# A hybrid attention and SSD layer on one core: TensorE's order in the SSD phase written out in the source, decay clamp moved to ScalarE

## The chip, the core and the metric

One NeuronCore of a Trainium2 chip runs the whole step. The metric is device time in microseconds, from three runs of the kernel before: 3272.0, 3275.4 (the median) and 3277.58. PE is TensorE's matmul, PEld its weight load, DVE VectorE, ACT ScalarE, POOL GpSimd, SP the queue from which all DMAs are issued here.

## The reference

The input is a prompt of 2048 tokens and a sample group of 8 x 8 tokens, width 1024. One projection of the normalised input gives queries, keys, values, gates and the SSD's inputs. Beside a windowed attention stands a Mamba-2 branch (4 groups of 8 heads, state 128), scanned in chunks of 128 tokens:

```python
a_cs = jnp.cumsum(dts * A, axis=2)
seg = a_cs[:, :, :, None] - a_cs[:, :, None]
Lm = jnp.exp(jnp.where(causal, seg, -jnp.inf))
cb = jnp.einsum('bclgn,bcsgn->bclsg', Cs, Bs)
y_diag = jnp.einsum('bclsg,bclsgh,bcsghp->bclghp', cb, Lm, dx)
states = jnp.einsum('bclgn,bclgh,bclghp->bcghpn', Bs, decay_to_end * dts, xs)
# h = h * chunk_decay + states, chunk after chunk
y_off = jnp.einsum('bclgn,bcghpn,bclgh->bclghp', Cs, h_prev, jnp.exp(a_cs))
```

x, B and C come from a causal convolution of width 4 and a silu; the SSD's output is multiplied by silu(z) and normalised by group. Both branches are projected, gated, added and projected once more.

## The kernel before, in words

The prompt is cut into 4 blocks of 512 tokens. Three phases follow each other in one program: `phase_t1` (norm, attention projections, attention), `phase_s` (SSD) and `phase_t2` (the gates, the output projections and the sample group's small work). Every fp32 operand of a projection is split into two fp32r parts, and three products of the parts are summed, so one output tile of 128 x 512 takes 8 x 3 matmuls (`proj_w`, L181).

`phase_s` goes over 16 pairs of block and group. For each, `proj_group` makes ten projection tiles: B, C, four of x (all six through `conv_tile`, whose L742 and L743 on ACT take a tile out of PSUM and whose three L748 on DVE do the convolution) and four of z (L814, L815). Block 0 carries the sample's 64 columns too; there each tile is two matmul streams of 288 columns in two of the three PSUM buffers `mm`. Weights are loaded for two tiles at a time by `wload`, rounded on ACT (L147) and subtracted on DVE (L148). `load_h` fetches a block's eight `hT` tiles.

`ssd_group` then does, for B and C of all four chunks, transposes (L826) and C by B (L832), and for each chunk: the decay matrix L (DMA of the sums to `AB`, eight DVE clamps L843, Exp L844 on ACT, times `cbm` on POOL L845); `po`, C by the carried state H (L854); transposes of x (L858), `dx` and `wx` (L861, L862); `py`, the product with L (L866); `ws` split on ACT and POOL (L868, L869); `st`, the chunk's state (L872); the new H on DVE (L879); the output (L881 to L885). A group ends with squares and their sum (L887 to L897). `dt_block` makes a block's step sizes by a softplus of some twenty small DVE operations and three matmuls (L767 to L769).

The order of instructions on each engine is not the source's: a planner with a cost model of its own lists them, on all engines and across phases. It lays SSD matmuls of one group between projection matmuls of the next, often in the middle of a tile, and it lays projections of block 0 between the last attention matmuls of `phase_t1`. Each engine runs its list strictly in that order, and an instruction whose input is late holds up all behind it.

Of the kernel before, what the change touches and what calls it, by code (L numbers as in the profile page):

```python
# [9 lines left out]
F32 = mybir.dt.float32  # L10
F32R = mybir.dt.float32r
AF = mybir.ActivationFunctionType
# [5 lines left out]
P = 128  # L18
# [57 lines left out]
def build(tc, nc, a, o, seq, phases=("T1", "S", "T2"), dbg=None):  # L76
# [629 lines left out]
    def phase_s():  # L706
        with ExitStack() as es:
# [50 lines left out]
            def dt_block(b):  # L758
# [5 lines left out]
                V.tensor_tensor(dA, dt, A_bc.unsqueeze(1).to_broadcast([P] + sh), ALU.mult)  # L764
                dA2 = dA.rearrange("p c h -> p (c h)")
# [17 lines left out]
            def proj_group(b, g, hT):  # L783
                xcp = xcps[(4 * b + g) % 2]
                xT = xcp.tile([P, 4, TB], F32, name="xT", tag="xT")
                BT = xcp.tile([P, TB], F32, name="BT", tag="BT")
                CT = xcp.tile([P, TB], F32, name="CT", tag="CT")
                zs = xcp.tile([P, 4, TB], F32, name="zs", tag="zs")
                cb, cc = OFF_B + P * g, OFF_C + P * g
                smp = b == sb  # L790
                _, hl = wload([(0, w_in[:, cb : cb + P]), (P, w_in[:, cc : cc + P])])
                st = sample_tile(smp)
                for i, (ct, out) in enumerate(((16 + g, BT), (20 + g, CT))):
                    pcs = prompt_pieces(proj_w(mmp, hl, i * P, hT, smp), st[:, i] if smp else None)
                    conv_tile(pcs, ct, out)
                    if smp:
                        SY.dma_start(xs_d[:, ct], st[:, i])
                for i in range(2):
                    c = 512 * g + 256 * i
                    _, hl = wload([(0, w_in[:, OFF_X + c : OFF_X + c + 256])])  # L800
                    st = sample_tile(smp)
                    for j in range(2):
                        pcs = prompt_pieces(proj_w(mmp, hl, j * P, hT, smp), st[:, j] if smp else None)
                        conv_tile(pcs, 4 * g + 2 * i + j, xT[:, 2 * i + j])
                    if smp:
                        SY.dma_start(xs_d[:, 4 * g + 2 * i : 4 * g + 2 * i + 2], st)
                for i in range(2):
                    c = 512 * g + 256 * i
                    _, hl = wload([(0, w_in[:, OFF_ZS + c : OFF_ZS + c + 256])])
                    st = sample_tile(smp)  # L810
                    for j in range(2):
                        th = cp.tile([P, TB], F32, name="th", tag="th")
                        for ps, lo, n in prompt_pieces(proj_w(mmp, hl, j * P, hT, smp), st[:, j] if smp else None):
                            A.activation(th[:, lo : lo + n], ps, AF.Tanh, scale=0.5)  # L814
                            V.scalar_tensor_tensor(  # L815
                                out=zs[:, 2 * i + j, lo : lo + n], in0=th[:, lo : lo + n], scalar=1.0, in1=ps,
                                op0=ALU.add, op1=ALU.mult,
                            )
                    if smp:
                        SY.dma_start(zs_d[:, 4 * g + 2 * i : 4 * g + 2 * i + 2], st)  # L820
                return xT, BT, CT, zs

            def ssd_group(b, g, xT, BT, CT, zs, dt, acs, dec, wd):
                tr = trp.tile([P, NT, P], F32, name="tr", tag="tr")
                for c in range(NT):
                    PE.transpose(tr[:, c], BT[:, c * P : (c + 1) * P], ident)  # L826
                Bt = ck.tile([P, 2, NT, P], F32R, name="Bt", tag="Bt", bufs=1)
                split(Bt[:, 0], Bt[:, 1], tr)
                pcb = trp.tile([P, NT, P], F32, name="tr", tag="tr")
                for c in range(NT):  # L830
                    sl = slice(c * P, (c + 1) * P)
                    PE.matmul(pcb[:, c], BT[:, sl], CT[:, sl], start=True, stop=True)  # L832
                cbm = ck.tile([P, NT, P], F32, name="cbm", tag="cbm")
                V.tensor_tensor(cbm, pcb, tri.unsqueeze(1).to_broadcast([P, NT, P]), ALU.mult)  # L834
                for c in range(NT):
                    first = b == 0 and c == 0
                    sl = slice(c * P, (c + 1) * P)
                    hc = slice(c * 32 + 8 * g, c * 32 + 8 * g + 8)
                    AB = lp.tile([P, 8, P], F32, name="AB", tag="AB")
                    SY.dma_start(AB.rearrange("p h l -> p (h l)"), ac_d[b][hc].rearrange("h l -> (h l)").partition_broadcast(P))  # L840
                    L = lp.tile([P, 8, P], F32, name="L", tag="L")
# [3 lines left out]
                    G.tensor_tensor(L, L, cbm[:, c].unsqueeze(1).to_broadcast([P, 8, P]), ALU.mult)  # L845
                    if not first:
                        EB = lp.tile([P, 4, P], F32, name="EB", tag="EB")
                        for hl in range(2):
                            src = ac_d[b][hc].rearrange("(i l) t -> l i t", l=2)[hl]
                            SY.dma_start(EB[64 * hl : 64 * hl + 64], src.partition_broadcast(64))  # L850
                        A.activation(EB, EB, AF.Exp)
                        po = yop.tile([P, 4, P], F32, name="po", tag="po")
                        for i in range(4):
                            PE.matmul(po[:, i], H[g][:, i * P : (i + 1) * P], CT[:, sl], start=True, stop=True)  # L854
                        V.tensor_tensor(EB, po, EB, ALU.mult)
                    tr = trp.tile([P, 8, 64], F32, name="tr", tag="tr")
                    for i in range(4):
                        PE.transpose(tr[:, 2 * i : 2 * i + 2].rearrange("p h d -> p (h d)"), xT[:, i, sl], ident)  # L858
                    dx = ck.tile([P, 8, 64], F32, name="dx", tag="dx")
                    wx = ck.tile([P, 8, 64], F32, name="wx", tag="wx", bufs=1)  # L860
                    V.tensor_tensor(dx, tr, dt[:, hc].unsqueeze(2).to_broadcast([P, 8, 64]), ALU.mult)  # L861
                    V.tensor_tensor(wx, tr, wd[:, hc].unsqueeze(2).to_broadcast([P, 8, 64]), ALU.mult)  # L862
                    py = yp.tile([P, 4, P], F32, name="py", tag="py")
                    for i in range(4):
                        for hl in range(2):
                            PE.matmul(py[64 * hl : 64 * hl + 64, i], dx[:, 2 * i + hl], L[:, 2 * i + hl], start=True, stop=True)  # L866
                    ws = ck.tile([P, 2, 8, 64], F32R, name="ws", tag="ws", bufs=1)
                    A.copy(ws[:, 0], wx)  # L868
                    G.tensor_tensor(ws[:, 1], wx, ws[:, 0].bitcast(F32), ALU.subtract)  # L869
                    pst_ = stp.tile([P, 8, 64], F32, name="st", tag="st")  # L870
                    for n, (x, y) in enumerate(SPLIT3):
                        PE.matmul(pst_, Bt[:, x, c], ws[:, y], start=n == 0, stop=n == 2)  # L872
                    Hg = H[g].rearrange("p (h d) -> p h d", h=8)
                    if first:
                        V.tensor_copy(Hg, pst_)
                    else:
                        hd = ck.tile([P, 8, 64], F32, name="hd", tag="hd", bufs=1)
                        G.tensor_tensor(hd, Hg, dec[:, hc].unsqueeze(2).to_broadcast([P, 8, 64]), ALU.mult)
                        V.tensor_tensor(Hg, pst_, hd, ALU.add)  # L879
                    u = xT[:, :, sl]  # L880
                    G.tensor_tensor(u, u, Dcol[:, 4 * g : 4 * g + 4].unsqueeze(2).to_broadcast([P, 4, P]), ALU.mult)  # L881
                    V.tensor_tensor(u, py, u, ALU.add)  # L882
                    if not first:
                        G.tensor_tensor(u, u, EB, ALU.add)
                    V.tensor_tensor(zs[:, :, sl], zs[:, :, sl], u, ALU.mult)  # L885
# [8 lines left out]
                for i in range(2):  # L894
                    PE.matmul(pss, onesr, thl[:, i], start=i == 0, stop=i == 1)
# [421 lines left out]
```

## Time and profile before

| | |
|---|---|
| median of three runs | 3275.4 us (3272.0 to 3277.58) |
| profiled execution | span 3273.9 us; no other time of this execution is known |
| PE, PEld | 3130.4 us (96%), 2656.9 us (81%) |
| DVE, ACT, POOL | 2234.8 (68%), 1308.2 (40%), 1045.0 us (32%) |
| granted TensorE clock | 0.987 on the mean |

The 1.5 us between the span and the median are what lies around the span, and scatter. The busy shares are means over three unlike phases. A busy PE is not a PE at its pace, since matmuls overlap and their ends are modelled; how fast a stretch runs is read from the starts of matmuls that follow each other.

### The profile page before, as it was taken

What the parts mean: (1) busy time and instruction counts of PE and PEld (TensorE: products, weight loads), DVE (VectorE), ACT (ScalarE), POOL (GpSimd) and SP (SyncE); (2) the same over time, 40 slices, a digit from 0 to 9 for tenths busy, and PEclk for the clock granted to TensorE, in tenths of its full rate; (3) what the DMA queues carried; (4) which work ended last, traced back from release to release, by engine and by line L of the source; (5) the groups of instructions that cost most, each with busy time, mean ns of one, the idle gap of its engine ahead of it and who ended that gap; (6) DMA issues with size and microseconds to landing.
All of it is one profiled execution on the core that took longest, in us unless ns stands there. A gap on an engine that the chain in (4) does not pass through costs nothing.

```text
span 3273.9 us, 49350 instructions
## 1 busy us (share of the span) xinstructions
PE 3130.4 (96%) x19038; PEld 2656.9 (81%) x19038; DVE 2234.8 (68%) x3777; ACT 1308.2 (40%) x2334; POOL 1045.0 (32%) x965
## 2 busy tenths in 40 slices
PE   6999999999989999998999999999999999999999
PEld 5978787878878877776777777788877799999888
DVE  3777768678887798989888898555555554334433
ACT  3555535456344344434444444332333333222322
POOL 1534343443445455556554555200211110000000
PEclk8999999999999999999999999999999999999999
DMA  6544425323433444444344433444764574345443
GB/s 210 156 134 124 128 73 169 106 70 124 130 122 110 154 125 135 126 156 133 116 143 155 127 118 119 154 141 117 229 184 142 131 226 147 97 135 168 132 116 101
DMA packets 472788, 448.76 MB, mean 137 GB/s; under 512 B 33808, under 2 KB 420520, under 8 KB 472504
## 3 DMA queue, kind: packets, MB, share of 16 engines
q1 hardware_dynamic: 472552, 445.60, 44.9%
q8 instruction: 150, 2.46, 0.3%
q14 instruction: 86, 0.70, 0.1%
HBM read 382.26 MB, written 65.35 MB: 137 GB/s over the span
## 4 chain that ended last, share of the span: by engine, by line
PE 63%; DVE 24%; DMA 5%; POOL 3%; issue 3%; ACT 2%; SPq 1%; DVEq 0%; ACTq 0%; POOLq 0%
PE mm L181 37%; PE mm L192 11%; DVE acc L748 5%; DVE L L843 5%; PE mm L168 5%; DVE whl L148 3%; PE tr L547 3%; PE sc L519 2%; POOL L L845 2%; DVE zs L885 1%; DMA v<-v_d 1%; PE tr L536 1%; DVE xT L882 1%; DVE H L879 1%; DMA hT<-h_d 1%
## 5 line engine op out<-in xcount | busy, mean ns | idle before, releaser
L181 PE MATMUL mm<-hT,whl 128*128 128x512 f32 (+1 forms) x6720 | 1353.7, 357 | 19.8 <-DMA hT<-h_d 9.9
L181 PEld LDWEIGHTS mm<-hT,whl 128*128 128x128 f32 x6720 | 1122.0, 190 | 194.0 <-issue 22.9
L148 DVE TENSOR_TENSOR whl<-raw,whl 128x2048 fp32r<-128x2048 f32 (+1 forms) x232 | 522.7, 2256 | 261.7 <-ACT whl L147 255.4
L181 PE MATMUL mm<-ot,whl 128*128 128x512 f32 (+1 forms) x2880 | 571.7, 356 | 1.2 <-DVE whl L148 0.8
L181 PEld LDWEIGHTS mm<-ot,whl 128*128 128x128 f32 x2880 | 476.1, 189 | 74.0 <-issue 5.7
L147 ACT CAST whl<-raw 128x2048 fp32r<-128x2048 f32 (+1 forms) x232 | 412.7, 1787 | 250.1 <-PE mm L181 133.9
L192 PE MATMUL mm<-whl,hT 128*128 128x256 f32 (+1 forms) x2304 | 305.6, 288 | 16.2 <-ACT whl L147 12.8
L192 PEld LDWEIGHTS mm<-whl,hT 128*128 128x128 f32 x2304 | 288.6, 190 | 24.4 <-ACT whl L147 13.0
L748 DVE SCALAR_TENSOR_TENSOR acc<-cr,cwb,acc 128x512 f32<-128x512 f32 x288 | 274.9, 960 | 10.4 <-ACT acc L743 5.0
L845 POOL TENSOR_TENSOR L<-L,cbm 128x1024 f32<-128x1024 f32 x64 | 200.2, 3138 | 115.3 <-DVE cbm L834 57.9
L192 PE MATMUL mm<-whl,ot 128*128 128x256 f32 (+1 forms) x1632 | 203.9, 284 | 0.0
L192 PEld LDWEIGHTS mm<-whl,ot 128*128 128x128 f32 (+1 forms) x1632 | 197.6, 188 | 5.3 <-issue 4.9
L168 PE MATMUL mm<-hT,whl 128*128 128x512 f32 x768 | 195.1, 403 | 6.0 <-DVE zs L418 3.7
L843 DVE TENSOR_SCALAR L<-AB,acs 128x128 f32<-128x128 f32 x512 | 192.0, 443 | 0.0
L168 PEld LDWEIGHTS mm<-hT,whl 128*128 128x128 f32 x768 | 142.6, 191 | 42.0 <-issue 5.2
L844 ACT ACTIVATE L<-L 128x1024 f32<-128x1024 f32 x64 | 67.8, 1062 | 187.8 <-DVE L L843 187.8
L365 ACT ACTIVATE s<-s,ng 128x128 f32<-128x128 f32 x256 | 100.0, 394 | 59.9 <-DVE ng L359 57.7
L147 ACT CAST ot<-v 128x512 fp32r<-128x512 f32 x96 | 59.0, 621 | 158.4 <-DVE v L1183 79.9
L752 ACT ACTIVATE th<-acc 128x512 f32<-128x512 f32 x96 | 60.6, 632 | 145.4 <-DVE acc L748 145.3
L869 POOL TENSOR_TENSOR ws<-wx,ws 128x512 fp32r<-128x512 f32 x64 | 102.5, 1601 | 44.4 <-ACT ws L868 44.4
L540 POOL TENSOR_TENSOR PT<-PT 128x512 f32<-128x512 f32 x60 | 78.2, 1308 | 92.6 <-DVE PT L539 78.9
L1183 DVE SCALAR_TENSOR_TENSOR v<-v,snw,rb 128x512 f32<-128x512 f32 x64 | 48.0, 770 | 84.7 <-DMA v<-v_d 84.7
(320 smaller groups left out, 3964.3 us busy)
## 6 DMA issues: line engine op xcount, KB each, us to landing
raw<-in_w_in_dram SPq DMA_DIRECT2D x120, 1024.0 KB
hT<-h_d SPq DMA_DIRECT2D x80, 512.0 KB
raw<-in_w_in_dram SPq DMA_DIRECT2D x64, 512.0 KB
AB<-ac_d SPq DMA_DIRECT2D x64, 512.0 KB
raw<-in_w_ssd_proj_dram SPq DMA_DIRECT2D x32, 1024.0 KB
v_d<-zs SPq DMA_DIRECT2D x16, 1024.0 KB
v<-v_d SPq DMA_DIRECT2D x64, 256.0 KB
raw<-in_w_attn_proj_dram SPq DMA_DIRECT2D x64, 256.0 KB
```

The costliest lines, as they stand in the source:

```text
L147: A.copy(hi, src)
L148: V.tensor_tensor(lo, src, hi.bitcast(F32), ALU.subtract)
L168: PE.matmul(ps, hl[:, x, k, c0 : c0 + P], ht[:, y, :], start=first and i == 0, stop=last and i == n - 1,)
L181: PE.matmul(ps, hl[:, x, k, c0 : c0 + P], ht[:, y, lo : lo + n], start=i == 0, stop=i == 3 * len(hT) - 1,)
L192: PE.matmul(ps, ht[:, x, tt * P : tt * P + m], hl[:, y, k, :n], start=i == 0, stop=i == 3 * len(hT) - 1,)
L365: A.activation(s[:, i, :width], s[:, i, :width], AF.Exp, bias=ng[:, i : i + 1], accum_out=den[:, i : i + 1])
L540: G.tensor_tensor(PT[:, 0], PT[:, 0], PT[:, 1], ALU.subtract)
L547: PE.matmul(po[64 * kvl : 64 * kvl + 64], vT[:, tt + w, kv * HD : (kv + 1) * HD], PTs[kvl][:, w], start=w == ws[0], stop=w == 1,)
L748: V.scalar_tensor_tensor(out=acc, in0=raw[:, k : k + TB], scalar=cwb[:, k, ct : ct + 1], in1=acc, op0=ALU.mult, op1=ALU.add)
L843: V.tensor_scalar(L[:, h], AB[:, h], acs[:, hc.start + h : hc.start + h + 1], 0.0, ALU.subtract, ALU.min)
L845: G.tensor_tensor(L, L, cbm[:, c].unsqueeze(1).to_broadcast([P, 8, P]), ALU.mult)
L869: G.tensor_tensor(ws[:, 1], wx, ws[:, 0].bitcast(F32), ALU.subtract)
```

## The change

One group's SSD work is cut into steps (`s_bc`, `s_decay`, `s_x`, `s_off`, `s_state`, `s_square`, `s_stats`), and a loop over groups and ten slots, one for each projection tile, puts a step ahead of a slot's projection. Steps 7 to 9 of a group stand in its own last slots, steps 10 to 19 in the slots of the next group. Inside `manual_schedule` PE's instructions keep the source's order; the other four engines are still listed by the planner, and so are PE's attention matmuls of the phase ahead. `dt_block` is cut in two, weights are asked for one pair of tiles ahead, and the clamp min(AB - acs, 0) on DVE becomes Relu(acs - AB) on ACT with Exp of its negative.

```diff
-                    for h in range(8):
-                        V.tensor_scalar(L[:, h], AB[:, h], acs[:, hc.start + h : hc.start + h + 1], 0.0, ALU.subtract, ALU.min)
-                    A.activation(L, L, AF.Exp)
...
+                for h in range(8):
+                    A.activation(L[:, h], AB[:, h], AF.Relu, scale=-1.0, bias=acs[:, hc.start + h : hc.start + h + 1])
+                A.activation(L, L, AF.Exp, scale=-1.0)
...
-            for b in range(NB):
-                dts_ = dt_block(b)
-                hT = load_h(b, b == sb)
-                for g in range(4):
-                    ssd_group(b, g, *proj_group(b, g, hT), *dts_)
-                    stats(b, g)
...
+            def weights(m):
+                if m < len(pairs):
+                    whl[m] = wload(pair_parts(*pairs[m]))[1]
+
+            def ssd_step(u, step):
...
+                if step == 7:
+                    t["dt"] = dts_[b]
+                    s_bc(t, b, g)
+                    s_decay(t, b, g, 0)
+                elif step >= 8 and step % 2 == 0:
+                    c = (step - 8) // 2
+                    if 0 < c <= NT:
+                        s_state(t, b, g, c - 1)
+                    if c < NT:
+                        s_x(t, b, g, c)
+                elif step >= 9 and step < 9 + 2 * NT:
+                    c = (step - 9) // 2
+                    s_off(t, b, g, c)
+                    if c + 1 < NT:
+                        s_decay(t, b, g, c + 1)
+                if step == 16:
+                    s_square(t, b, g)
+                if step == 19:
+                    s_stats(t, b, g)
+
+            weights(0)
+            half = dt_block(0)
+            with tc.manual_schedule(engines={mybir.EngineType.PE}):
+                for u, (b, g) in enumerate(groups):
+                    if g == 0:
+                        hT = load_h(b, b == sb)
+                    ts[u] = tiles(u)
+                    for slot in range(10):
+                        if slot % 2 == 0:
+                            m = 5 * u + slot // 2
+                            weights(m + 1)
+                            st = sample_tile(b == sb)
+                        if slot == 5 and u == 0:
+                            dts_[0] = dt_sums(0, *half)
...
+                        ssd_step(u - 1, slot + 10)
+                        ssd_step(u, slot)
+                        project(ts[u], b, g, slot, whl[m], hT, st)
+            for step in range(10, 20):
+                ssd_step(len(groups) - 1, step)
```

`s_off` holds `po` (L883 now), its product, the sum into u and the decayed state `hd`; `s_state` holds `st` (L895), the new H, `py` (L904) and the output; `s_x` the transposes (L864), `wx`, `dx` and `ws`. `project` is one projection tile, `dt_sums` the three matmuls of the step sizes (L770 to L772) and what follows.

The first place is PE in a middle group of blocks 1 to 3, before:

```order
L858 MATMUL tr<-cst,xT 128x128 x4
L181 MATMUL mm<-hT,whl 128x512 x6
L866 MATMUL py<-L,dx 64x128 x8
L872 MATMUL st<-ws,Bt 128x512
L858 MATMUL tr<-cst,xT 128x128 x4
L181 MATMUL mm<-hT,whl 128x512
L872 MATMUL st<-ws,Bt 128x512 x2
L181 MATMUL mm<-hT,whl 128x512 x13
```

And the same work after it:

```order
L181 MATMUL mm<-hT,whl 128x512 x24
L895 MATMUL st<-ws,Bt 128x512 x3
L904 MATMUL py<-L,dx 64x128 x8
L864 MATMUL tr<-cst,xT 128x128 x4
L181 MATMUL mm<-hT,whl 128x512 x24
L883 MATMUL po<-CT,H_8612 128x128 x4
L181 MATMUL mm<-hT,whl 128x512 x24
L895 MATMUL st<-ws,Bt 128x512 x3
```

Between `st` and the `po` that reads the new H there is now always one whole projection tile of 24 matmuls.

The second place is PE where attention ends (L519, L536, L547) and the SSD phase has begun, before:

```order
L536 MATMUL tr<-cst,s 128x128 x4
L181 MATMUL mm<-hT,whl 128x288 x13
L547 MATMUL tr<-PT,vT 64x512
L181 MATMUL mm<-hT,whl 128x288 x47
L547 MATMUL tr<-PT,vT 64x512 x3
L181 MATMUL mm<-hT,whl 128x288 x128
L767 MATMUL tr<-dA,cst 128x128
```

And after:

```order
L181 MATMUL mm<-hT,whl 128x288 x32
L519 MATMUL sc<-KTT,qT 128x256 x4
L547 MATMUL tr<-PT,vT 64x512
L519 MATMUL sc<-KTT,qT 128x256 x4
L547 MATMUL tr<-PT,vT 64x512 x3
L536 MATMUL tr<-cst,s 128x128 x4
L519 MATMUL sc<-KTT,qT 128x256 x8
L536 MATMUL tr<-cst,s 128x128
L547 MATMUL tr<-PT,vT 64x512
L536 MATMUL tr<-cst,s 128x128 x11
L547 MATMUL tr<-PT,vT 64x512 x7
L770 MATMUL tr<-dA,cst 128x128
```

Before, 575 projection matmuls (L181) stand ahead of the step sizes' three; after, 240, and the last 32 of them stand ahead of all that is left of the attention.

The third place is the two halves of a tile in block 0, PE with buffer numbers (one number is one half), before:

```order
L181 MATMUL mm_9603<-hT_8688,whl_9599 128x288 x3
L181 MATMUL mm_9603<-hT_8692,whl_9599 128x288 x3
L181 MATMUL mm_9604<-hT_8664,whl_9599 128x288 x3
L181 MATMUL mm_9604<-hT_8668,whl_9599 128x288 x3
L181 MATMUL mm_9604<-hT_8672,whl_9599 128x288 x3
```

And after:

```order
L181 MATMUL mm_9126<-hT_8665,whl_8970 128x288
L181 MATMUL mm_9127<-hT_8665,whl_8970 128x288
L181 MATMUL mm_9126<-hT_8665,whl_8970 128x288
L181 MATMUL mm_9127<-hT_8665,whl_8970 128x288
L181 MATMUL mm_9126<-hT_8669,whl_8970 128x288
```

The planner ran one half out before the other; now they alternate from the first matmul, so a tile needs both its buffers at once.

## Rows read from the trace of the kernel before

**Rows 1.** Four stretches: length, busy PE PEld DVE ACT POOL, clock, DMA, GB/s.
```profile
737.30:843.10 105.80, 105.65 (x721) 93.19 (x722) 85.91 (x187) 55.81 (x164) 27.15 (x40) 0.98 0.37 118
843.10:1398.60 555.50, 516.85 (x3254) 449.54 (x3253) 478.17 (x759) 240.65 (x341) 289.61 (x229) 0.98 0.42 129
1398.60:2020.80 622.20, 575.94 (x3038) 464.23 (x3037) 552.17 (x789) 269.16 (x341) 336.48 (x270) 0.98 0.43 136
2020.80:2072.50 51.70, 40.82 (x240) 32.44 (x239) 43.35 (x55) 18.98 (x23) 32.95 (x19) 0.90 0.47 144
```
**Rows 2.** PE's waits, 843 to 2087: us in all, times, longest.
```profile
PE po L854 <- DVE H L879: 37.4, 29, 4.2
PE st L895 <- DVE thl L891: 14.3, 9, 2.5
PE mm L181 <- DMA hT<-h_d: 7.4, 2, 3.8
```
**Rows 3.** PE in order of time, 1500 to 1600: start, length, instructions.
```profile
1504.23 0.94 PE L872 MATMUL st<-ws,Bt 128*128 128x512 f32 x3
1505.01 5.64 PE L181 MATMUL mm<-hT,whl 128*128 128x512 f32 x24
...
1547.43 15.60 PE L181 MATMUL mm<-hT,whl 128*128 128x512 f32 x68
1562.87 0.60 PE L826 MATMUL tr<-cst,BT 128*128 128x128 f32 x4
1563.31 1.06 PE L832 MATMUL tr<-CT,BT 128*128 128x128 f32 x8
1564.20 1.06 PE L854 MATMUL po<-CT,H 128*128 128x128 f32 x8
1565.01 4.59 PE L181 MATMUL mm<-hT,whl 128*128 128x512 f32 x19
...
1574.77 1.09 PE L866 MATMUL py<-L,dx 128*64 128x128 f32 x16
1575.79 0.50 PE L872 MATMUL st<-ws,Bt 128*128 128x512 f32 x1
```
**Rows 4.** PE in order of time, where attention has ended.
```profile
826.01 17.26 PE L181 MATMUL mm<-hT,whl 128*128 128x288 f32 x128
843.11 0.38 PE L767 MATMUL tr<-dA,cst 128*128 128x128 f32 x2
```
**Rows 5.** DVE's clamp in the third stretch, grouped: busy us, mean ns, idle before.
```profile
L843 DVE TENSOR_SCALAR L<-AB,acs 128x128 f32<-128x128 f32 x256 | 97.1, 448 | 0.0
```
**Rows 6.** ACT over the whole span, grouped by form.
```profile
L365 ACT ACTIVATE s<-s,ng 128x128 f32<-128x128 f32 x256 | 100.0, 394 | 59.9 <-DVE ng L359 57.7 <-DVE den L367 1.8
L844 ACT ACTIVATE L<-L 128x1024 f32<-128x1024 f32 x64 | 67.8, 1062 | 187.8 <-DVE L L843 187.8
L743 ACT ACTIVATE acc<-mm,cwb 128x288 f32<-128x288 f32 x24 | 14.3, 596 | 5.7 <-DVE xT L753 3.4 <-DVE CT L753 2.1
L742 ACT COPY cr<-mm 128x288 f32<-128x288 f32 x24 | 9.5, 395 | 19.0 <-PE mm L181 19.0
```
**Rows 7.** ACT in order of time, a 128 x 128 activation.
```profile
827.05 0.31 ACT L692 ACTIVATE e<-x 128x128 f32<-128x128 f32 x1 [4.15 <-DVE x L691]
```
**Rows 8.** DVE from 733 to 844, grouped by form.
```profile
L748 DVE SCALAR_TENSOR_TENSOR acc<-cr,cwb,acc 128x512 f32<-128x512 f32 x21 | 18.9, 898 | 0.0
L148 DVE TENSOR_TENSOR whl<-raw,whl 128x2048 fp32r<-128x2048 f32 x7 | 16.5, 2352 | 5.6 <-ACT whl L147 5.6
```
**Rows 9.** DVE in order of time: softplus first and last, first clamp.
```profile
826.73 0.28 DVE L691 TENSOR_TENSOR x<-dt,dtb_bc 128x128 f32<-128x128 f32 x1
...
839.79 0.29 DVE L764 TENSOR_TENSOR dA<-dt,A_bc 128x128 f32<-128x128 f32 x1
...
850.05 1.66 DVE L843 TENSOR_SCALAR L<-AB,acs 128x128 f32<-128x128 f32 x8
```
**Rows 10.** PE in block 0, a tile that waits for its buffer.
```profile
969.20 1.15 PE L181 MATMUL mm<-hT,whl 128*128 128x288 f32 x5 [1.77 <-ACT acc L743]
```

More of the change, by code (lines that the diff above doesn't have):

```diff
@@ L781, in dt_block, with pair_parts @@
                 return dt.rearrange("p c h -> p (c h)"), acs, dec, wd
[L783 to L789, printed above, removed]
-                smp = b == sb
[L791 to L794, printed above, removed]
+            def pair_parts(b, g, n):
+                if n == 0:
+                    cb, cc = OFF_B + P * g, OFF_C + P * g
+                    return [(0, w_in[:, cb : cb + P]), (P, w_in[:, cc : cc + P])]
+                c = (OFF_X if n < 3 else OFF_ZS) + 512 * g + 256 * ((n - 1) % 2)
+                return [(0, w_in[:, c : c + 256])]
@@ new lines, in tiles, with project @@
+            def tiles(u):
+                xcp = xcps[u % 2]
+                return dict(
+                    x=xcp.tile([P, 4, TB], F32, name="xT", tag="xT"), B=xcp.tile([P, TB], F32, name="BT", tag="BT"),
+                    C=xcp.tile([P, TB], F32, name="CT", tag="CT"), z=xcp.tile([P, 4, TB], F32, name="zs", tag="zs"),
+                )
+            def project(t, b, g, slot, hl, hT, st):
+                smp = b == sb
+                n, j = slot // 2, slot % 2
+                pcs = prompt_pieces(proj_w(mmp, hl, j * P, hT, smp), st[:, j] if smp else None)
+                i = 2 * ((n - 1) % 2) + j
+                if n == 0:
+                    ct, out = ((16 + g, t["B"]), (20 + g, t["C"]))[j]
@@ L807, in proj_group @@
[L807 to L820, printed above, removed]
@@ new lines, in s_off @@
+            def s_off(t, b, g, c):
+                if not (b or c):
+                    return
+                dt, acs, dec, wd = t["dt"]
+                hc, sl = heads(g, c), slice(c * P, (c + 1) * P)
+                EB = t["EB", c]
+                po = yop.tile([P, 4, P], F32, name="po", tag="po")
+                for i in range(4):
+                    PE.matmul(po[:, i], H[g][:, i * P : (i + 1) * P], t["C"][:, sl], start=True, stop=True)
+                V.tensor_tensor(EB, po, EB, ALU.mult)
+                u = t["x"][:, :, sl]
+                G.tensor_tensor(u, u, EB, ALU.add)
+                hd = t["hd", c] = ck.tile([P, 8, 64], F32, name="hd", tag="hd", bufs=1)
+                Hg = H[g].rearrange("p (h d) -> p h d", h=8)
+                G.tensor_tensor(hd, Hg, dec[:, hc].unsqueeze(2).to_broadcast([P, 8, 64]), ALU.mult)
@@ new lines, in s_state @@
+            def s_state(t, b, g, c):
+                sl = slice(c * P, (c + 1) * P)
+                pst_ = stp.tile([P, 8, 64], F32, name="st", tag="st")
+                for n, (x, y) in enumerate(SPLIT3):
+                    PE.matmul(pst_, t["Bt"][:, x, c], t["ws", c][:, y], start=n == 0, stop=n == 2)
+                Hg = H[g].rearrange("p (h d) -> p h d", h=8)
+                if b or c:
+                    V.tensor_tensor(Hg, pst_, t["hd", c], ALU.add)
+                else:
+                    V.tensor_copy(Hg, pst_)
+                py = yp.tile([P, 4, P], F32, name="py", tag="py")
+                for i in range(4):
+                    for hl in range(2):
+                        PE.matmul(
+                            py[64 * hl : 64 * hl + 64, i], t["dx", c][:, 2 * i + hl], t["L", c][:, 2 * i + hl],
+                            start=True, stop=True,
+                        )
+                u, z = t["x"][:, :, sl], t["z"][:, :, sl]
+                V.tensor_tensor(u, py, u, ALU.add)
+                V.tensor_tensor(z, z, u, ALU.mult)
```

141 lines of the change are left out of this document (73 added, 68 removed).

## The prediction

> **What bounds the kernel now.** I read the stretches first. The SSD phase runs from 737.3, where its first projection starts, to 2072.5, where its last matmul ends; I cut it where the first step sizes are summed (843.1), at the last group of block 1 (1398.6, its L826) and at the last group of all (2020.8). In the third stretch, eight whole groups, PE is busy 575.9 us of 622.2 and DVE 552.2, so 93% and 89%, while ACT has 43% and POOL 54% [rows 1]. So two engines are nearly full. The PE row says busy where it isn't at its pace, so I build PE's floor from starts. 68 projection matmuls of 512 columns take 1562.87 - 1547.43 = 15.44 us, 0.227 each; a group's 240 take 54.5. Four transposes take 0.44, C by B 0.89, `po` 0.81, `py` 1.02, `st` 0.78 [rows 3]. A chunk is then 0.81 + 0.44 + 1.02 + 0.78 = 3.05, four are 12.2, and with the two jobs for B and C and two matmuls of `st`'s shape for the squares (0.52) a group's SSD is 14.05. The floor of a group is 68.6 us. With 0.7 for each of two step-size sums, eight groups need 550 us; they took 622.2. Excess: 72 us, 9 a group.
>
> Block 0's matmuls of 288 columns take (843.11 - 826.01) / 128 = 0.134 [rows 4]. The second stretch has 1345 of these (1920, less the 575 ahead of the step sizes), 960 of 512 columns, seven groups' SSD and two sums: 180 + 218 + 98 + 1 = 497 of 555.5, excess 58. In the fourth stretch one group's SSD without B and C (12.7), some 83 gate matmuls of the next phase (18.9) and 17 transposes (some 2) make 34 of 51.7, excess 18. The first stretch has PE busy 105.65 of 105.8 [rows 1]: excess 0. Together 148 us, all that the change can take from here.
>
> Then I read whom PE waits for. `po` waits for the new H 29 times, 37.4 us in all; the squares' matmul waits 14.3 for DVE; 7.4 go to the `hT` loads at two block starts [rows 2]. The chain behind the first is `st`, DVE's H, `po`; it is late because the planner puts `po` too soon behind `st`, and because DVE is full. The named waits explain less than half of the excess. The rest lies in a clock of 0.98 and 0.90 [rows 1], of the two levels 1.2 and 2.4 GHz the lower one after such waits, and in matmuls that run late without a named wait.
>
> **The change part by part.**
>
> *Steps between tiles (third stretch).* PE's work stays the same, only its order moves. Between `st` and the `po` that needs H now stand `py`, four transposes and 24 projection matmuls, 1.02 + 0.44 + 5.5 = 7 us, against one DVE operation. `ws` and L have two slots, about 14 us. So these waits go. What is late next? DVE loses its clamps: 552.2 - 97.1 [rows 1, 5] leaves 455 us of the new length of some 565, 81%, so it no longer ends last. ACT gains 256 Relus of 128 x 128. The trace has no Relu; the nearest rows are an activation of that size at 0.31 [rows 7] and one that also sums, 0.394 [rows 6]. I take 0.31: +79 us (at 0.394: +101), ACT 348 to 370 of 565, 62 to 65%. It runs beside PE and costs nothing as long as evacuations of PSUM aren't held up; three `mm` buffers cover two slots, 11 us, against a block of eight Relus and an Exp of 3.5 to 4.2 us. Block starts remain: `hT` is freed only by the last tile of the old block, about 3 us each (the two rows' mean is 3.7, and 2.2 us of SSD now stand between). I leave 1 us a group for late operands and 3 for each of two block starts: 14 in place of 72, a gain of 58. Ends: 4 (0 a group, 2 a start) and 46 (5 a group).
>
> Against the Relus speaks the Trainium skill, ScalarE: Activation LUTs, Rules for kernel authors: relu belongs on VectorE, which is faster for each element. Here DVE's clamp takes 448 ns on the mean and ACT's activation of that size 310, so the trace does not bear that out in this stretch. By the page's price, 280 ns and 0.833 ns an element less 93 for back-to-back issue, 256 Relus would be an estimated 75 us, and the sum stays.
>
> *Halves that alternate (block 0).* A tile takes two of three `mm` buffers, and its second half needs the buffer that the first half of the tile before has just filled. PE then waits for ACT's two evacuations, 0.395 + 0.596 = 1.0 [rows 6], unless an SSD step stands between. In the trace such a wait was 1.77 behind transposes of 0.44 [rows 10], so 2.2. I take 1.2, near the row without a queue on ACT. Group 0 has eight slots with little cover: 9 us. Groups 1 to 3 have three odd slots covered by `po` alone (0.4 each) and one by transposes alone (0.8): 2 each, 6. With 1 a group for block 1 and 3 for its start: 15 + 4 + 3 = 22 in place of 58, gain 36. Ends: 11 in place of 15 at 1.0, 40 at 2.2.
>
> *The join with attention (first stretch).* Here the change costs. PE's list has 335 fewer projection matmuls ahead of the step sizes, 45 us less cover, so PE comes there at 798 in place of 843. But the sums stand behind all of the attention in PE's list, and need the softplus on DVE. DVE was 86 of 106 us busy [rows 1]; it loses four weight splits at 2.35 and five convolutions at 0.9 [rows 8], 14 us, and some 4 of small work, so the attention that ended at 826 ends near 808. Softplus took 13.1, with 5 of other work in it [rows 9]; alone some 8. The sums come at 816, PE waits 18 (up to 27 if the softplus keeps its 13 and more). Behind them, ACT's list has 16 Relus and an Exp ahead of the next evacuation: data came 6.9 us after the sums (843.1 to 850.05 [rows 9]), then 5.0 + 1.1 + 1.0, while PE has 0.7 + 6.4 us of work that doesn't need it: 7 more. A loss of 25, between 15 and 40.
>
> *The tail.* Its steps are the planner's again; without DVE's clamps I take 15 in place of 18, gain 3 (-2 to 8).
>
> *Phase 1.* The planner's lists move there too, with the same instructions. Nothing in the trace prices it: 0, between -10 and +10.
>
> Sum: 58 + 36 - 25 + 3 = 72. From the span, 3273.9 - 72 = 3201.9; with the 1.5 us by which the median of three stands above it, **3203 us**.
>
> **The rivals.** *More than that* (0.11): operands are never late, ends at their good side: 68 + 40 - 15 + 8 = 101, 3174, and down to 3158 with a better phase 1. For it: DVE falls to 81%. Against it: the join cannot be free.
>
> *A rigid list* (0.12): the planner still orders the other four engines by its own costs, so PE's fixed list meets late operands as before. If the 29 waits for H stay in other places (37) and block 0 waits 2.2 a slot (25 more), 3265. For it: a third of the excess is such waits today. Against it: every operand now has a slot of 5.5 us at least.
>
> *ScalarE ends last* (0.07, slower): Relus stand ahead of evacuations in ACT's single list, and wait for their DMA there. A block of eight at 0.394 and its Exp is 4.2 us; if each of 64 chunks passes 1.4 us of it on to PE, that is 90, 3293. It decides from 72 / 64 = 1.1 us a chunk. Against it: 62 to 65% busy, and two slots of buffers in blocks 1 to 3. For it: block 0 has no such buffers. The Trainium skill's rule on relu, quoted above, would make this the likelier case.
>
> **How the numbers follow.** My forecast has 0.70, with its own range 3170 to 3240. Within 0.2% (6.5 us, about what a measurement of this kernel can tell from no change) lies the upper end of the rigid list, 0.03. Slower: 0.07. Faster: 0.70 + 0.11 + 0.09 = 0.90. The range that holds 8 in 10 leaves out ScalarE's case and the ends of the two others: 3156 to 3262.
>
> **What would show it.** The waits of `po` for H fall from 37.4 to under 5. Group to group, `L828` to `L828`, 69 to 71 us in blocks 2 and 3 in place of 77.8. PE waits once, 15 to 27 us, ahead of L770. In block 0 PE waits for L743's `acc` in most slots, 0.4 to 1.2 each. ACT stands at 60 to 66% there, DVE near 80%. It is wrong if a group takes over 75 us, if DVE or ACT has no idle time in the third stretch, or if phase 1 ends elsewhere by over 10 us.

## The result, and the profile after

The changed kernel takes 3365.1 us (median; 3362.9 to 3370.0) against 3274.0 us of the kernel before (now four runs, 3272.0 to 3277.6): ratio 1.0283, 95% interval 1.027 to 1.0295. It is slower by 91 us, where 3203 us was forecast. The profiled execution has a span of 3361.1 us, 87.2 above before.

The same four stretches as [rows 1], cut at the first B transposes (L828 now), the first of group 7, those of the last group, and a point as far from the end as 2072.5 was before. Columns: length, busy PE, PEld, DVE, ACT, POOL, clock, DMA share, GB/s.

```profile
737.30:846.20 108.90, 82.08 (x488) 67.33 (x489) 80.33 (x190) 57.21 (x171) 26.69 (x39) 0.87 0.38 120
846.20:1424.20 578.00, 537.25 (x3419) 469.38 (x3418) 436.14 (x507) 294.04 (x558) 275.06 (x226) 0.97 0.38 119
1424.20:2095.20 671.00, 599.24 (x3032) 476.72 (x3031) 507.91 (x531) 341.09 (x599) 323.19 (x273) 0.94 0.41 126
2095.20:2160.00 64.80, 56.52 (x303) 44.40 (x302) 45.56 (x51) 31.55 (x53) 34.38 (x22) 0.92 0.46 143
```

The third stretch has the same eight groups as before: 671.0 us in place of 622.2, 83.9 a group. No engine is full (PE 89%, DVE 76%, ACT 51%). Of the 48.8 us more, 25.5 are idle time of PE and 23.3 are busy time for nearly the same number of instructions (3032, 3038 before). The granted clock fell from 0.98 to 0.94: it stood at the lower of its two levels (1.2 of 2.4 GHz) more often. So the loss is waiting, and slower matmuls beside it.

Those waits of the changed kernel from 843 to 2087 us that bear on this (total, times, longest), and the Relus, which replace the clamps of [rows 5] (busy us, mean ns, idle before):

```profile
ACT th L752 <- DVE acc L748: 216.9, 70, 5.3
ACT EB L857 <- DMA EB<-ac_d: 185.5, 54, 9.9
PE tr L864 <- DVE xT L753: 35.4, 11, 5.4
PE st L895 <- POOL ws L871: 23.8, 18, 2.1
PE tr L864 <- DVE cbm L836: 16.5, 9, 2.9
PE st L895 <- ACT ws L870: 9.4, 9, 1.2
PE po L883 <- DVE H L898: 2.3, 5, 0.5
```
```profile
L853 ACT ACTIVATE L<-AB,acs 128x128 f32<-128x128 f32 x512 | 156.7, 396 | 4.2 <-DMA AB<-ac_d 4.2
```

The wait that the change was to remove, `po` for H, is gone (37.4 to 2.3, [rows 2]), and a Relu costs what was forecast: 156.7 us for 512 are 0.306 each (one by itself lasts 396 ns on the mean, but they overlap). In its place PE waits for x, `cbm` and `ws`, 85 us in all. The view that names the cause is ACT's: its Exp of EB (the decay from the chunk's start, loaded into one of two buffers and then multiplied by `po`) waits 185.5 us for EB's load. ACT's longer wait, of the tanh L752 for the convolution, is not the cause: e9 below keeps it (212.4 us) and is faster than before. In the trace of before the row for EB was

```profile
ACT EB L851 <- DMA EB<-ac_d: 59.6, 36, 7.8
```

The chain of waits through one chunk (start, length, what) shows how that reaches PE:

```profile
1655.74 1.77 POOL xT L886
1657.53 0.58 SPq L851
1658.11 0.05 issue
1658.16 2.94 DMA EB<-ac_d
...
1661.21 0.12 ACT EB L857
...
1661.75 0.56 ACT cr L742
1662.31 0.69 ACT acc L743
1663.03 1.15 DVE acc L748
...
1670.43 0.69 DVE EB L884
...
1671.25 1.67 POOL xT L886
1672.93 0.58 SPq L851
```

It is a loop. GpSimd's addition (L886) frees one of two EB buffers; SyncE issues the load into it; ACT's Exp, which the planner has put into ACT's list right there, 37 us ahead of its use on the median of the 60 chunks, waits for the load; the evacuation of the next tile (L742, L743) stands behind it; VectorE's convolution follows, behind it in VectorE's list the next chunk's product of EB with `po` (L884), and then the next addition. Issues follow each other at 1621.74, 1637.27, 1657.53 and 1672.93, after 15.5, 20.3 and 15.4 us. PE's own step, two tiles and a chunk, takes 14.2 where nothing is late (`st` at 1636.62 and 1650.78). Of each period 3.6 to 4.9 us are the load and its issue; without them, if all else stayed, it would be an estimated 11.9, 15.3 and 11.8.

The Exp did not stand nearer to its buffer's release than before the change: on the median of all chunks it starts 5.7 us behind the addition that frees the buffer, and 5.8 in the trace of before. What is new is that ACT has come to it and waits, 54 times for 3.4 us on the mean in place of 36 times for 1.7, with the next tile's evacuation behind it.

ACT and then PE in order of time, behind one such Exp (start, length, instruction, idle before and releaser):

```profile
1661.21 0.63 ACT L857 ACTIVATE EB<-EB 128x512 f32<-128x512 f32 x1 [2.49 <-DMA EB<-ac_d]
1661.75 0.56 ACT L742 COPY cr<-mm 128x512 f32<-128x512 f32 x1
1662.21 0.78 ACT L743 ACTIVATE acc<-mm,cwb 128x512 f32<-128x512 f32 x1
1662.88 1.91 ACT L147 CAST whl<-raw 128x2048 fp32r<-128x2048 f32 x1
1664.69 2.45 ACT L853 ACTIVATE L<-AB,acs 128x128 f32<-128x128 f32 x8
1667.04 0.61 ACT L870 CAST ws<-wx 128x512 fp32r<-128x512 f32 x1
```
```profile
1661.01 5.72 PE L181 MATMUL mm<-hT,whl 128*128 128x512 f32 x24
1667.70 0.50 PE L895 MATMUL st<-ws,Bt 128*128 128x512 f32 x1 [0.96 <-ACT ws L870]
1670.02 0.73 PE L895 MATMUL st<-ws,Bt 128*128 128x512 f32 x2 [1.82 <-POOL ws L871]
1670.68 1.60 PE L904 MATMUL py<-L,dx 128*64 128x128 f32 x16
1672.21 6.82 PE L181 MATMUL mm<-hT,whl 128*128 128x512 f32 x24
```

Once the Exp could go, ACT worked without a gap down to `ws`, 6.4 us later, and PE's `st` waited for both halves of `ws`, 2.8 us. The tile behind it took 6.82 us in place of 5.72; the granted clock was 0.83 there, 1.00 in the tile ahead. The Relus are in this list, but they did not make it late: the Exp in front of them did.

### The profile page after: what moved, and what is told of

It reads as the page before. It is cut to its first block, busy times and chain, and to the rows that moved or that the text cites. A ratio compares the mean times of both kernels' runs of the same rounds, so it can differ in the third digit from the quotient of the medians.

```text
span 3361.1 us, 49467 instructions
## 1 busy us (share of the span) xinstructions
PE 3165.0 (94%) x19038; PEld 2677.7 (80%) x19038; DVE 2144.3 (64%) x3265; ACT 1445.7 (43%) x2846; POOL 1012.4 (30%) x965
## 3 DMA queue, kind: packets, MB, share of 16 engines
q8 instruction: 149, 2.44, 0.3%
## 4 chain that ended last, share of the span: by engine, by line
PE 57%; DVE 13%; DMA 11%; ACT 8%; issue 5%; POOL 4%; SPq 2%; ACTq 0%; POOLq 0%; DVEq 0%
PE mm L181 33%; PE mm L192 11%; DMA EB<-ac_d 5%; PE mm L168 4%; DVE whl L148 3%; PE tr L547 2%; POOL xT L886 2%; ACT whl L147 2%; ACT L L853 2%; DVE acc L748 2%; PE sc L519 1%; DMA raw<-in_w_in_dram 1%; DMA ss_d<-sm 1%; DMA hT<-h_d 1%; ACT acc L743 1%
## 5 line engine op out<-in xcount | busy, mean ns | idle before, releaser
L181 PE MATMUL mm<-hT,whl 128*128 128x512 f32 (+1 forms) x6720 | 1388.6, 363 | 36.2 <-DMA hT<-h_d 15.1
L181 PEld LDWEIGHTS mm<-hT,whl 128*128 128x128 f32 x6720 | 1139.1, 194 | 217.7 <-DMA hT<-h_d 21.3
L148 DVE TENSOR_TENSOR whl<-raw,whl 128x2048 fp32r<-128x2048 f32 (+1 forms) x232 | 507.6, 2191 | 245.5 <-ACT whl L147 244.8
L181 PE MATMUL mm<-ot,whl 128*128 128x512 f32 (+1 forms) x2880 | 569.9, 355 | 0.3 <-DVE whl L148 0.3
L181 PEld LDWEIGHTS mm<-ot,whl 128*128 128x128 f32 x2880 | 475.2, 189 | 72.3 <-issue 5.7
L748 DVE SCALAR_TENSOR_TENSOR acc<-cr,cwb,acc 128x512 f32<-128x512 f32 x288 | 333.9, 1159 | 93.1 <-ACT acc L743 89.7
L192 PEld LDWEIGHTS mm<-whl,hT 128*128 128x128 f32 x2304 | 290.6, 191 | 28.4 <-DVE zs L418 15.3
L855 POOL TENSOR_TENSOR L<-L,cbm 128x1024 f32<-128x1024 f32 x64 | 168.2, 2638 | 31.8 <-DVE cbm L836 30.6
L871 POOL TENSOR_TENSOR ws<-wx,ws 128x512 fp32r<-128x512 f32 x64 | 128.6, 2009 | 151.4 <-ACT ws L870 151.4
L168 PEld LDWEIGHTS mm<-hT,whl 128*128 128x128 f32 x768 | 141.8, 190 | 39.2 <-DVE zs L418 3.3
L853 ACT ACTIVATE L<-AB,acs 128x128 f32<-128x128 f32 x512 | 156.7, 396 | 4.2 <-DMA AB<-ac_d 4.2
L752 ACT ACTIVATE th<-acc 128x512 f32<-128x512 f32 x96 | 60.5, 630 | 224.8 <-DVE acc L748 220.7
L857 ACT ACTIVATE EB<-EB 128x512 f32<-128x512 f32 x60 | 37.9, 632 | 206.0 <-DMA EB<-ac_d 197.6
L886 POOL TENSOR_TENSOR xT<-xT,EB 128x512 f32<-128x512 f32 x60 | 94.6, 1577 | 63.4 <-DVE EB L884 58.8
L746 POOL COPY carry<-cr 128x3 f32<-128x3 f32 x96 | 49.7, 517 | 204.7 <-ACT cr L742 204.7
```

What stands on the lines that cost most here:

```text
L148: V.tensor_tensor(lo, src, hi.bitcast(F32), ALU.subtract)
L168: PE.matmul(ps, hl[:, x, k, c0 : c0 + P], ht[:, y, :], start=first and i == 0, stop=last and i == n - 1,)
L181: PE.matmul(ps, hl[:, x, k, c0 : c0 + P], ht[:, y, lo : lo + n], start=i == 0, stop=i == 3 * len(hT) - 1,)
L192: PE.matmul(ps, ht[:, x, tt * P : tt * P + m], hl[:, y, k, :n], start=i == 0, stop=i == 3 * len(hT) - 1,)
L748: V.scalar_tensor_tensor(out=acc, in0=raw[:, k : k + TB], scalar=cwb[:, k, ct : ct + 1], in1=acc, op0=ALU.mult, op1=ALU.add)
L853: A.activation(L[:, h], AB[:, h], AF.Relu, scale=-1.0, bias=acs[:, hc.start + h : hc.start + h + 1])
```

## The experiments

Theory: this loop. Rivals: the Relus in ACT's list (A), PE's fixed list by itself (B), SyncE's list (C), and, from e8 on, that ACT's wait is slack once the load is gone (D) and that the transfers as such cost (E). Times are medians; each group of experiments had its own runs of before (3272.7, 3274.4 and 3275.9 us).

| kernel | us | ratio to before, 95% interval |
|---|---|---|
| e1 changed, clamp on VectorE again | 3427.6 | 1.0471 (1.0455 to 1.0487) |
| e2 changed, planner orders PE | 3285.6 | 1.0042 (1.0028 to 1.0056) |
| e3 before, Relus alone | 3220.0 | 0.9840 (0.9825 to 0.9855) |
| e4 changed, EB from AB | 3243.8 | 0.9910 (0.9895 to 0.9925) |
| e5 changed, three EB buffers | 3369.1 | 1.0290 (1.0273 to 1.0308) |
| e6 before, Relus, EB from AB | 3210.8 | 0.9803 (0.9788 to 0.9818) |
| e7 as e2, EB from AB | 3198.7 | 0.9766 (0.9751 to 0.9780) |
| e8 as e4, three EB buffers | 3245.1 | 0.9911 (0.9896 to 0.9926) |
| e9 changed, Exp of EB late | 3240.1 | 0.9885 (0.9864 to 0.9906) |
| e10 as e4, PE fixed from group 1 on | 3232.2 | 0.9865 (0.9849 to 0.9882) |
| e11 as e2, Exp of EB late | 3193.6 | 0.9745 (0.9726 to 0.9764) |

**e1, the Relus undone.**

```diff
-                    A.activation(L[:, h], AB[:, h], AF.Relu, scale=-1.0, bias=acs[:, hc.start + h : hc.start + h + 1])
-                A.activation(L, L, AF.Exp, scale=-1.0)
+                    V.tensor_scalar(L[:, h], AB[:, h], acs[:, hc.start + h : hc.start + h + 1], 0.0, ALU.subtract, ALU.min)
+                A.activation(L, L, AF.Exp)
```

> The changed kernel with one part undone: the clamp of the decay is eight VectorE operations a chunk again instead of eight ScalarE Relus; TensorE's fixed order stays. Theory (a loop through ScalarE's list: the Exp of EB stands in the list ahead of evacuations of PSUM and waits for EB's load, which in turn waits for GpSimd to have freed one of two EB buffers and stands behind other transfers in SyncE's list): the Relus are not the cause, the Exp of EB still waits over 150 us in the SSD phase and the time stays at 3330 to 3380 us. Rival A (the Relus: 2.4 us a chunk in ScalarE's list): ScalarE's list gets 157 us shorter and the time falls to 3200 to 3270 us.

3427.6 us, 62 slower than with the Relus. Rival A falls by its sign. The theory was right that the Relus are not the cause, but it missed their use: it had left the time where it was. The Exp's wait for the load in the SSD phase was 135 us, where it had forecast over 150.

**e2, PE's order left to the planner** (`with tc.manual_schedule(...)` taken out).

> The changed kernel without the fixed order on TensorE: the planner orders its instructions, as before the change; the source's new order of steps and the Relus stay. Theory (loop through ScalarE's list by EB's load): the loop does not depend on TensorE's order; TensorE can take other work while it waits, so some comes back, but not all: 3290 to 3350 us, the Exp of EB waiting over 120 us. Rival B (the rigid list by itself, any late operand stops TensorE): the loss goes with it, 3240 to 3285 us, TensorE's waits for xT, cbm and ws under 20 us together.

3285.6 us: 79 of the 91 come back, just past the theory's range and at the edge of B's. B's condition did not hold, though: late operands still cost PE 77 us, nearly what they cost under the fixed order.

```profile
ACT EB L857 <- DMA EB<-ac_d: 176.4, 50, 10.7
PE st L895 <- POOL ws L871: 28.1, 19, 2.5
PE tr L864 <- DVE xT L753: 25.6, 12, 2.3
PE tr L864 <- DVE cbm L836: 15.7, 10, 3.2
PE st L895 <- ACT ws L870: 7.9, 9, 1.2
```

The Exp waits about as long as under the fixed list, so the loop comes with the new order of the source, whoever orders PE; the fixed list makes it dearer (e6 and e7 give the sizes). Neither forecast was right alone.

**e3, the Relus without the rest.** The same lines as in e1, the other way round, in the kernel before.

> The kernel before with one part of the change alone: the eight clamps of a chunk on ScalarE as Relus, nothing else. Theory (loop through ScalarE's list by EB's load): the Relus alone cost little, VectorE is relieved by 97 us in a stretch where it is at 88%: 3240 to 3290 us. Rival A (the Relus hold ScalarE's list): 3310 to 3370 us.

3220.0 us, 53 faster than before, and beyond the theory's better end (3240). In the old order the Relus are all gain. Its third stretch, and the wait that the new order was to remove:

```profile
1370.40:1960.80 590.40, 570.07 (x3038) 461.77 (x3037) 475.67 (x533) 341.33 (x597) 344.82 (x270) 0.99 0.45 143
```
```profile
PE po L854 <- DVE H L879: 9.0, 14, 1.6
```

With VectorE relieved of its clamps, 28 of the 37 us that PE waited for H go in the old order of the source.

**e4, no load for EB.** ACT takes its Exp from the rows of AB that are on chip already, in two halves of 64 partitions.

```diff
-                    for hl in range(2):
-                        src = ac_d[b][hc].rearrange("(i l) t -> l i t", l=2)[hl]
-                        SY.dma_start(EB[64 * hl : 64 * hl + 64], src.partition_broadcast(64))
...
-                    A.activation(EB, EB, AF.Exp)
+                    for hl in range(2):
+                        rows = slice(64 * hl, 64 * hl + 64)
+                        A.activation(EB[rows], AB[rows].rearrange("p (i l) t -> p l i t", l=2)[:, hl], AF.Exp)
```

> The changed kernel, but EB (the decay from the chunk's start, broadcast) is no longer loaded by two transfers a chunk: ScalarE takes its Exp straight from the rows of AB that are there already, in two operations on 64 partitions each. Nothing is left out. Theory (loop through ScalarE's list by EB's load): the 186 us that ScalarE waited for EB's load go, TensorE's waits for xT, cbm and ws fall to under half of their 88 us, and at least the 88 us lost come back: 3220 to 3285 us. Rival A (the Relus and ScalarE's load): one operation more a chunk, so no gain or a loss of up to 30 us: 3360 to 3395 us. Rival B (TensorE's rigid list): small gain, 3330 to 3360 us.

3243.8 us, 121 better than the changed kernel. PE's waits for x, `cbm` and `ws` fall from 85 to 21 us. One thing came otherwise: ACT's wait did not go, it only changed its name, to the addition that frees the buffer.

```profile
ACT EB L855 <- POOL xT L884: 191.5, 58, 6.6
PE tr L862 <- DVE xT L753: 19.8, 12, 2.8
```

As long a wait of ACT cost 121 us with the load in the loop and nothing that shows without it. I read it so that what decides is the length of the loop beside PE's step, not how long an engine on it stands. The times of the additions fit: between 1618 and 1680 us they follow each other after 15.6, 15.8 and 14.7 us here, 15.9, 15.9 and 14.0 in e9, which is as fast, and 17.9, 19.8 and 15.5 in the changed kernel. No run changes the loop's length alone.

**e5, three EB buffers** (`bufs=3` for EB, `bufs=1` for `cbm` to make room).

> The changed kernel with three EB buffers in place of two, EB still loaded by its two transfers a chunk; the 2 KB come from the second buffer of cbm. Theory (the loop: EB's load waits for GpSimd to free a buffer, ScalarE's Exp of EB waits for the load, and the evacuations behind it in ScalarE's list wait with it): with a buffer more the load starts about 11 us, two projection tiles, earlier, ScalarE's wait for it falls from 188 us to under 60, and the time to 3240 to 3300 us. Rival C (SyncE's list: EB's load stands behind the statistics' transfers and the weights, whatever buffers there are): the wait stays over 120 us and the time at 3330 to 3370 us.

No change, 3369.1 us, and the wait is 194.2 us. The theory failed here as it was put: the planner used the buffer to put the Exp more than another chunk ahead in ACT's list (57 us ahead of its use on the median, in place of 37), again right behind the addition that frees its buffer. Rival C, which forecast this time, is met by e9, where SyncE's list keeps all of its transfers.

**e6 and e7, EB from AB in the two other orders.** The edit of e4 in e3 and in e2.

> The kernel before with two things alone: the Relus for the clamp, and EB's Exp taken from AB's rows in place of its own load; TensorE's order is the planner's, in the source order of before. ScalarE waited 41 us for EB's load with the Relus alone (3220 us), TensorE's waits in the SSD phase sum to 45 us. Theory (EB's load is a fault only where the order lets ScalarE's list hold TensorE up): little to win, 3195 to 3222 us. If the load costs through the DMA queues themselves, in any order: under 3190 us. If the 64 further operations on ScalarE cost: 3225 to 3245 us.

> The changed kernel without TensorE's fixed order and with EB taken from AB: the new source order of steps, the Relus, the planner's order on TensorE. With the fixed order this gave 3244 us, and the planner's order with EB's load 3286 us. Theory (EB's load through ScalarE's list is the larger part of the loss in both orders): 3190 to 3235 us, ScalarE's wait for EB under 60 us. Rival B (TensorE's rigid list is what EB's load acted through, and the planner had already worked around it): 3260 to 3285 us.

3210.8 and 3198.7 us. EB's load costs 9 us in the old order of steps (e3 to e6), 87 in the new one under the planner (e2 to e7) and 121 under the fixed list (changed to e4). In e7 ACT's wait for EB stayed, at 178.5 us for the addition, as in e4, where the theory had it under 60.

**e8, EB from AB and three buffers** (e4 with e5's buffers).

> The changed kernel with EB taken from AB and three EB buffers (the 2 KB from the second buffer of cbm). With two buffers ScalarE still waited 191 us for GpSimd's addition that frees the buffer, and a group took 75.2 us. Theory (that wait stands ahead of evacuations and so reaches TensorE): the wait falls under 60 us, a group comes to 70 to 73 us and the time to 3165 to 3220 us. Rival D (with the load gone the wait of ScalarE is slack; what is left at TensorE, 20 us for xT and the rest, comes from VectorE's list): 3235 to 3250 us.

3245.1 us, as e4 and as rival D had it. The wait itself stayed, though, 172 us for the addition, so this run does not yet show that it is slack; e9, with 43 us of it and the same time, does.

**e9, the Exp of EB at its own chunk.** Load, buffers and transfers stay; a column of zeros from the chunk's `wx` keeps the planner from placing the Exp far ahead of its use: 3.4 us on the median, 8.7 at most. (It had stood further ahead than the two tiles named below, at 37 us.)

```diff
-                    A.activation(EB, EB, AF.Exp)
...
+                    zc = ck.tile([P, 1], F32, name="zc", tag="zc")
+                    G.tensor_scalar(zc, wx[:, 0, 0:1], 0.0, None, ALU.mult)
+                    A.activation(EB, EB, AF.Exp, bias=zc)
```

> The changed kernel with EB still loaded by its two transfers into two buffers, but the Exp of EB tied to the chunk in which it is used: it takes as bias a column of zeros that GpSimd writes from wx of the same chunk, so that the planner can't put it into ScalarE's list earlier than that (it stood two projection tiles ahead, right behind the addition that frees its buffer). One GpSimd operation on 128x1 a chunk more. Theory (the load's 3 to 4 us matter only because the Exp stands in ScalarE's list at a place where the load has just been issued): ScalarE's wait for EB's load falls from 188 us to under 40, TensorE's waits for xT, cbm and ws to under half of 76 us, the time to 3225 to 3265 us, as with EB taken from AB. Rival E (the transfers themselves, 16 MB and 120 issues in SyncE's list, are what cost): 3320 to 3365 us.

3240.1 us, 125 better than the changed kernel and as fast as e4 within the scatter (3235.0 to 3243.6, e4 3238.0 to 3247.7), with every transfer still there. Rivals C and E fall: it is the place of the Exp in ACT's list. The planner may have moved other instructions with it; e4, which comes to the same time by another way, speaks against these as the cause. ACT's wait for the convolution (L752) is as long as in the changed kernel and costs nothing that shows. The waits, and the second and third stretch of e9:

```profile
ACT th L752 <- DVE acc L748: 212.4, 76, 5.1
ACT EB L871 <- POOL zc L870: 43.2, 16, 4.9
PE tr L862 <- DVE xT L753: 17.0, 9, 2.8
```
```profile
851.70:1390.00 538.30, 521.53 (x3417) 460.55 (x3416) 436.06 (x511) 300.49 (x566) 292.67 (x252) 1.00 0.42 127
1390.00:1979.00 589.00, 569.15 (x3032) 460.56 (x3031) 497.55 (x529) 340.66 (x593) 344.38 (x303) 0.99 0.47 144
```

Against the changed kernel the third stretch is 82 us shorter: 52 of idle time (71.8 to 19.9) and 30 of busy time for the same 3032 instructions, at a clock of 0.99 in place of 0.94. So 0.6 us of busy time went with each us of waiting; between the kernel before and the changed one it was 0.9 (23.3 and 25.5), so this is no fixed price.

**e10, the first group left to the planner** (the fixed order entered at group 1, EB from AB).

> The changed kernel with EB taken from AB (3244 us) and TensorE's order fixed from the second group on only: the first group's projections are again placed by the planner between the attention's last steps. Theory for the join: with the fixed order 336 projection matmuls stood ahead of the first transposes of B at 850 us, with the planner all 480 at 844 us; 144 matmuls of 0.134 us and 6 us are 25 us, of which up to 15 us may be given back because the first chunk's steps now follow each other with nothing between them: 3215 to 3238 us. Rival: the fixed order costs in the steady groups and not at the join: 3240 to 3255 us.

3232.2 us, 12 better than e4, in the theory's range: part of the fixed list's price lies at the join with attention. The first chunk's steps stood uncovered here (PE waits 10 us in them, from 843 to 860 us), so 12 is no upper bound for the join.

**e11, Exp late, planner's order on PE.**

> The new source order and the Relus with the planner's order on TensorE, EB loaded as before the change, and the Exp of EB tied to its own chunk by the column of zeros. Theory (place of the Exp in ScalarE's list): as with EB taken from AB under the planner's order, 3195 to 3225 us. Rival E (the transfers themselves): 3260 to 3290 us, as without the tie.

3193.6 us, just below the range, and the lowest median here: ratio 0.9745 to before. Again no price of the transfers shows: e7, which is without them, takes 3198.7.

## Why the prediction was wrong

The step that failed is the claim on the third stretch that waits go because "`ws` and L have two slots", with ACT's new work costing "nothing as long as evacuations of PSUM aren't held up". I weighed the Relus against three `mm` buffers and did not ask what else stands in ACT's list ahead of evacuations once the order changes. That was the Exp of EB, with 3.6 to 4.9 us of issue and load on the way from the buffer's release to it. In place of waits that go, PE waited 85 us for x, `cbm` and `ws`, and 121 to 125 us come back when the load (e4) or the early Exp (e9) goes. The row was in the trace of before, 59.6 us, and I passed over it because PE did not wait there.

Point by point, on the profiled executions:

- **The join.** Forecast a loss of 25, between 15 and 40. At L828 PE is 2.5 us later and 239 matmuls of 0.134 us [rows 4] behind (336 done against 575): 34.5. The waits are where the prediction put them, ahead of L770 (8.4; forecast 15 to 27, some 10 more fell into attention's last steps) and for ACT's evacuation (5.4; forecast 7). Attention ended at 815 and not at 808, and the sums came at 823.6 and not at 816.

```profile
823.58 0.80 PE L770 MATMUL tr<-dA,cst 128*128 128x128 f32 x2 [8.39 <-DVE dA L764]
...
824.88 8.15 PE L181 MATMUL mm<-hT,whl 128*128 128x288 f32 x49
838.46 7.96 PE L181 MATMUL mm<-hT,whl 128*128 128x288 f32 x47 [5.42 <-ACT acc L743]
846.25 0.60 PE L828 MATMUL tr<-cst,BT 128*128 128x128 f32 x4
```

- **Block 0 and block 1.** Forecast a gain of 36. The stretch took 578.0 in place of 555.5, with 15.7 us more of projections in it (239 of block 0 more, 72 of block 1 fewer), so it lost 7. In e9 it took 538.3: a gain of 33. The waits that the prediction put on the alternating halves, 15 us, did not come: PE waited for L743's `acc` three times, 2.8 us in all. By the prediction's own terms, too, its 40 us at 2.2 a slot are some 35, and the rigid list's 3265 is 3260.
- **The third stretch.** Forecast a gain of 58, ends 26 and 68; it lost 49. In e9 it gained 33, inside the ends. What then stays above the forecast are waits for x (17 us in the phase) and the tile itself: between SSD steps 24 matmuls take 5.54 to 5.58 us start to start, 1 us a group more than 0.227 each [rows 3].
- **The tail.** Forecast a gain of 3, ends -2 and 8. It took 64.8 with three tiles (16.3 us) more: 48.5 against 51.7. Some ten of the next phase's matmuls (2.3 us) had left it, so about 1 us is a gain, inside the ends.
- **The Relus.** Forecast 0.31 us each; eight take 2.44, and ACT stood at 51% where 60 to 66% were forecast, because the stretch was longer. Alone they gave 53 us. The prediction's comparison with the clamp, 448 ns against 310, took a mean of unlike times: eight clamps took 1.66 us [rows 9], less than eight Relus. In the trace of before 323 of the 512, with no GpSimd instruction beside them, lasted 0.27 to 0.29 us, and some of the others up to 1.52. The Trainium skill's reason for its rule on relu, which the prediction quotes (ScalarE: Activation LUTs, Rules for kernel authors), is given for bf16 operands; these are fp32, and VectorE's single operation is the shorter one here too. So the gain comes from taking work off the fuller engine (VectorE 89%, ACT 43% [rows 1]).
- **What the order itself gave.** The Relus alone (e3) gained some 28 us in block 0 and block 1 (526.5) and 32 in the third stretch (590.4); the new order on top of them, with the Exp late (e9), comes to 33 and 33. So nearly all of what came of the 58 and the 36 us is VectorE's relief, and I had put it down to the order in the main.
- **The rivals.** "ScalarE ends last", at 0.07, came nearest: its place was right (ACT's list, ahead of evacuations, waiting for a load) and so was its side; its instruction was wrong. It named the Relus, whose load was hardly waited for (4.2 us). "A rigid list" counts for 45 us (e4 to e7) of the 79 between the changed kernel and e2; the other 34 are the same list making the loop dearer. But of the 45 most is the join, not late operands in the groups: e7 comes to its first L828 at 844.3 us with 575 projection matmuls done, e4 at 849.8 with 336, which is 37.5 us; the third stretch takes 582.4 and 589.9.

The changed kernel's 91 us are then: Relus, a gain (53 alone in the old order, 62 in the new); the late EB in the fixed list, a loss of 121 to 125; and what is left of order and join, a loss of 24 against e3 even when EB is cured (3244 against 3220). In the traces of e3 and e4 this last part is a loss of 38 at the join (843.9 and 849.8 us at the first transposes of B, with 239 matmuls still to do), of which 4 come back in block 0 and block 1, nothing in the third stretch (590.4 and 589.9) and 9 in the tail. How to avoid the join's price under a fixed list stays open: e10, which leaves the first group to the planner, got 12 us back.

## What to carry to other kernels

Before an order is fixed on one engine, read the waits of the engines that feed it, also those that cost nothing yet: an instruction that waits for a transfer in an in-order list holds everything behind it, and moving work makes that visible. Follow the loop from a buffer's release to the next release and compare its length with the step of the bounding engine; a long wait inside a loop that is shorter can be slack (e4 against e9), and another buffer doesn't help where the planner spends it on going earlier (e5). Time the parts of a change apart: here one was worth 53 us and the other hid it.

## What the runs showed of the hardware

The same VectorE operation took very different times. In one stretch of the changed kernel (VectorE, then GpSimd, in order of time):

```profile
1601.23 0.74 DVE L748 SCALAR_TENSOR_TENSOR acc<-cr,cwb,acc 128x512 f32<-128x512 f32 x1
...
1604.38 2.83 DVE L753 SCALAR_TENSOR_TENSOR xT<-th,acc 128x512 f32<-128x512 f32 x1
1607.13 0.67 DVE L818 SCALAR_TENSOR_TENSOR zs<-th,mm 128x512 f32<-128x512 f32 x1
```
```profile
1603.94 5.51 POOL L855 TENSOR_TENSOR L<-L,cbm 128x1024 f32<-128x1024 f32 x2 [0.63 <-DVE cbm L836]
```

L753, with both inputs in SBUF, took 2.83 us beside GpSimd's multiply; L818, with one input in PSUM, 0.67 beside the same multiply; L748, of L753's form, 0.74 without GpSimd. The Trainium skill says so (SBUF — State Buffer, Who interferes with whom): a VectorE instruction with two SBUF inputs contends with a GpSimd instruction that reads SBUF, and one with at most one such input, outside VectorE's 2-port modes, doesn't. These rows agree with it, and so does the whole trace: 10 of these L753 beside that multiply took 2.83 us, 52 beside no GpSimd instruction 0.68 to 0.69, and 10 L818 beside the multiply 0.67 to 0.68. The last of PE's four transposes waited 2.80 us for the L753 shown. No run here took GpSimd's multiply away, so what it costs the kernel is open.
